# A two-layer hybrid decoder: the weight sums of the last projection made earlier and kept in DRAM, and a written order for all engines in it

## The chip, the core and the metric

The kernel runs on one core of a Trainium2 chip. A core has a tensor engine (PE, whose weight loads the profile lists as PEld), a vector engine (DVE), a scalar engine (ACT), a general engine (POOL) and a queue engine (SP) that here only issues DMAs. The metric is the device time of one execution in microseconds; lower is better.

## The reference

Two layers (`DEPTH` 2) over 1024 tokens of width 1024, in float32:

```
h    = rms_norm(x, pre_gain) * (1 + scale) + shift      # shift, scale, gate from SiLU(c) @ W_mod
proj = h @ w_in                                         # 3088 columns
A    = sliding_window_attention(...) * silu(ag)         # window 128, 8 heads, columns 0..511 of the mix
B    = rms_norm(retention(...)) * silu(rg)              # 4 heads, chunks of 128, columns 512..767
C    = rms_norm(gated_linear_attention(...)) * silu(gg) # 4 heads, columns 768..1023
x    = x + gate * rms_norm(concat(A, B, C) @ w_out, post_gain)
```

Each group of heads carries a state from chunk to chunk in B and C. The layers follow each other, and the last projection, `concat(A, B, C) @ w_out` of the second layer, ends the program.

## The kernel before

**Tiles.** Tokens are taken in 8 tiles of 128. Every matrix product of activations is made in three passes of a high and a low half (`PASSES`), so a product of one tile with a block of 512 rows and 512 columns has 12 matmuls of 128x512. The mix (A, B, C of a tile) is turned and written to DRAM in two halves (`mixS`), and for tiles 2 to 7 of the last layer also unsplit (`mixF`).

**Order of the work.** PE runs in the order in which the program is written (`manual_schedule` over PE). Everything that is not a long product is a *job*, a generator that yields delays. A counter `clk` adds up an assumed cost of the matmuls, and `pump()`, called between groups of matmuls, lets those jobs go on whose delay (from the table `L`) or flag is past. So `L` sets where a job's matmuls stand in PE's order. The other engines get an order from the framework's scheduler, unlike PE. SP's queue works in order, too; a DMA also waits for the one that was issued eight before it on its queue to land.

**The second layer** goes: gate projections, retention (`ret_core`, with the state `stR` on DVE), gated linear attention (`gla_core`, with the state `stG`), window attention in eight pairs of tiles (`attn_run`, `attn_two`: scores to PSUM, softmax on DVE, ACT and POOL in one of four `smx` tiles, transposes, values), the attention's gates (`gate`), and `last_output`.

**The last output.** Tiles 0 and 1 (`PLAIN` = 2) are multiplied block by block. The other six go in three pairs, an even and an odd tile, with seven products a pair instead of eight (a Strassen-like scheme). For it `w_out` is cut in 2 x 2 blocks of 512 x 512. The blocks W00, W10 and W11 are used as they are, and T1 to T4 are sums of blocks. Likewise sums of the two tiles' halves are made (L1430 to L1433) and split in high and low (`msplit`, L157 and L1404). The products of a pair come in the order W00, W10, T2, T1, W11, T3, T4. Results pass through three PSUM banks named `mm` and are added on DVE (L1470) to kept ones (`kept`, L1466 on ACT). Then come the square (L1474), the product with the gate (L1475), and `finish`, which reloads x, adds it (L1373) and stores the output.

**Weight sums.** T1 is made while it is loaded: two loads and a difference (L593) for each of four rows of blocks, `k`. T2, T3 and T4 are made in `sw_second`, a job that starts with the first product of tile 0: four loads, three sums on DVE (L591, L593, L621) and three splits (ACT copies, L157; DVE or POOL differences, L586) for each `k`. Staging tiles `st` are a ring of five.

```
for k in range(4):
    s3, x = sw_load(k, 0, 1), sw_load(k, 1, 1)
    sw_diff(s3, 1, k, x, s3)
    s2, s4 = sw_load(k, 0, 0), sw_load(k, 1, 0)
    eng("sd").tensor_tensor(s2, s3, s2, ALU.add)
    ...
```

Of the kernel before, what the change touches and what calls it, by code (L numbers as in the profile page):

```python
# [14 lines left out]
ALU = mybir.AluOpType  # L15
# [78 lines left out]
def trunk(ctx: ExitStack, tc: tile.TileContext, ins, cst, out):  # L94
# [66 lines left out]
    def dma(k, dst, src):  # L161
        {"S": nc.sync, "A": A, "P": G}[EN[k]].dma_start(dst, src)
# [5 lines left out]
    clk = [0.0]  # L168
    jobs = []
# [100 lines left out]
    srS = dr.tile([NT, P, 256], F32, name="srS")  # L270
    tabS = dr.tile([NP_, P, 2, 256], F32, name="tabS")
# [316 lines left out]
    def sw_diff(dst, i, k, x, y):  # L588

        if i and k > 1:  # L590
            V.scalar_tensor_tensor(dst, x, gnc[:, DEPTH - 1:DEPTH], y, ALU.mult, ALU.subtract)  # L591
        else:
            eng("sd").tensor_tensor(dst, x, y, ALU.subtract)  # L593

    def sw_first(name):
        def conv(k, x, y=None):
            if y is not None:
                sw_diff(x, 0, k, x, y)
# [9 lines left out]
        for k in range(4):  # L608
            if name == "T1":
                request(DEPTH - 1, 2, lambda k=k: (sw_load(k, 0, 1), sw_load(k, 0, 0)), lambda *s, k=k: conv(k, *s))  # L610
            else:
                i, j = int(name[1]), int(name[2])
                request(DEPTH - 1, 1, lambda k=k: (sw_load(k, i, j),), lambda *s, k=k: conv(k, *s))

    def sw_second():
        drain()
        for k in range(4):
            s3, x = sw_load(k, 0, 1), sw_load(k, 1, 1)
            sw_diff(s3, 1, k, x, s3)
            s2, s4 = sw_load(k, 0, 0), sw_load(k, 1, 0)  # L620
            eng("sd").tensor_tensor(s2, s3, s2, ALU.add)  # L621
            sw_split("T2", k, s2, "t2")
            sw_split("T3", k, s3, "t3")
            sw_diff(s4, 1, k, s4, s2)
            sw_split("T4", k, s4, "t4")
            yield L["sw1"]
        for name in ("T2", "T3", "T4"):
            flag(("sw", name))
# [38 lines left out]
    mark = [None] * 4  # L667
# [711 lines left out]
    def prod(dst, a, name, start=True, stop=True, c=slice(0, 512)):  # L1379

        w = sw(name)
        await_flag(("sw", name))
        q = 0
        for i, j in PASSES:
            for k in range(4):
                mult(dst, a[:, i, k, :], w[:, j, k, c], start and q == 0, stop and q == 11)
                q += 1
        pump()

# [11 lines left out]
    def msplit(slot, x, key):  # L1401
        xv = x.rearrange("p (k q) -> p k q", k=4)
        copy("mh" + key, slot[:, 0], xv)
        eng("ml" + key).tensor_tensor(slot[:, 1], xv, f(slot[:, 0]), ALU.subtract)  # L1404

    def slots(b):
        return b[:, :, 0:4, :], b[:, :, 4:8, :]

    class Pair:

        def __init__(self, l, p):
            self.l, self.e, self.o = l, 2 * p, 2 * p + 1

        def parts(self):
            l, e, o = self.l, self.e, self.o
            need_mix(l, e)
            need_mix(l, o)
            self.p = mpart(o, 0), mpart(o, 1), mpart(e, 0), mpart(e, 1)

        def sum(self):  # L1420
            e = self.e
            self.a = []
            for c in range(2):
                s = gp.tile([P, NT * P], F32R, tag=f"kT{c}", name=nm("ma"), bufs=1).rearrange(
                    "p (a k q) -> p a k q", a=2, k=4)
                for a in range(2):
                    dma("lmix", f(s[:, a]), mixS[e, :, a, 4 * c:4 * c + 4])
                self.a.append(s)
            a21, a22, a11, a12 = self.p
            eng("ms0").tensor_tensor(a22, a21, a22, ALU.add)  # L1430
# [404 lines left out]
```

## Time and profile before

| what | value |
|---|---|
| three runs | 992.6, 993.15, 996.84 us; median 993.15 |
| the profiled execution | 1000.45 us, its span 998.7 us |
| granted TensorE clock, mean | 0.982 |
| PE busy | 951.3 us |
| DVE, ACT, POOL busy | 690.3, 414.6, 273.5 us |
| second layer's retention and gated attention | about 590 to 790 us |
| window attention and gates | about 790 to 903 us |
| last output | 898 to 998.7 us; PE's last matmul ends at 991.0 |
| HBM read, written | 109.2 MB, 36.2 MB |

The page lists busy time by engine, then the costliest groups of instructions by source line, with the idle time before them and what ended it. Matmuls are pipelined and their ends are modelled. In the rows of a timeline the bracket names the idle time of the engine before that row and the instruction that ended it; `L173` and `L188` are helpers in which all matmuls and transposes are recorded, `L157` and `L159` one for copies, `L162` one for DMAs.

### The profile page before, as it was taken

Reading aid. Unit: us, or ns where it says so; the run is one execution under the profiler, and the core shown is the slowest. Engines: PE = TensorE matmul, PEld = TensorE weight load, DVE = VectorE, ACT = ScalarE, POOL = GpSimd, SP = SyncE. Lnnn points to the kernel's source line nnn. Section 1 sums busy time; section 2 is a strip of 40 time slices with the busy share of each in tenths; the row PEclk is TensorE's granted clock in tenths of the full one; section 3 lists DMA queues with packets and bytes.
Section 4 is the critical chain, followed back from the end, with each engine's and each line's share of the span. In section 5 each row is a group of like instructions: output and inputs, shape, how many; then the busy total and the mean of one; then the engine's idle time right before and its main releaser. Section 6 shows DMA issues by size and latency. Waiting matters only on the chain. (4 is left out here: it accounts for less than half of the span.)

```text
span 998.7 us, 19555 instructions
## 1 busy us (share of the span) xinstructions
PE 951.3 (95%) x7117; PEld 829.5 (83%) x7117; DVE 690.3 (69%) x1679; ACT 414.6 (42%) x1160; POOL 273.5 (27%) x302
## 2 busy tenths in 40 slices
PE   5788999999999999999999999999999998999796
PEld 1687999988998877878889999998899876777575
DVE  4788956857756777755677385785766568866876
ACT  3677521223332556633455431133333256663322
POOL 1776101222430234420123010122331034634001
PEclk9899999989999999999999999999999999999899
DMA  9742623433326255687455150361223324587874
GB/s 296 272 129 81 189 73 103 135 97 94 117 83 183 71 171 165 187 272 257 164 172 170 59 165 32 118 179 65 68 78 101 111 86 133 163 267 206 263 240 143
DMA packets 129968, 148.76 MB, mean 149 GB/s; under 512 B 14112, under 2 KB 94284, under 8 KB 129872
## 3 DMA queue, kind: packets, MB, share of 16 engines
q1 hardware_dynamic: 124176, 137.96, 45.5%
q10 hardware_dynamic: 5696, 9.56, 2.6%
q8 instruction: 56, 0.92, 0.4%
q14 instruction: 40, 0.33, 0.1%
HBM read 109.20 MB, written 36.18 MB: 146 GB/s over the span
## 5 line engine op out<-in xcount | busy, mean ns | idle before, releaser
L173 PE MATMUL mm<-arena,arena 128*128 128x256 f32 (+2 forms) x2880 | 463.6, 316 | 4.4 <-POOL arena L553 1.4
L173 PEld LDWEIGHTS mm<-arena,arena 128*128 128x128 f32 x2880 | 401.7, 190 | 38.6 <-ACT arena L722 2.5
L657 POOL TENSOR_TENSOR sm<-sm,mhalf 128x1 f32<-128x1 f32 (+1 forms) x64 | 55.4, 867 | 326.4 <-DVE sm L656 320.0
L173 PE MATMUL mm<-arena,mx 128*128 128x512 f32 (+1 forms) x564 | 130.6, 388 | 6.2 <-ACT kept L1466 4.8
L173 PE MATMUL mm<-arena 128*128 128x256 f32 (+2 forms) x768 | 126.7, 317 | 6.2 <-DVE arena L723 3.4
L173 PEld LDWEIGHTS mm<-arena,mx 128*128 128x128 f32 x564 | 103.2, 191 | 28.6 <-ACT kept L1466 5.3
L173 PEld LDWEIGHTS mm<-arena 128*128 128x128 f32 x768 | 108.7, 191 | 16.4 <-DVE arena L723 4.1
L553 POOL TENSOR_TENSOR arena<-st,arena 128x512 fp32r<-128x512 f32 x34 | 51.0, 1503 | 104.0 <-ACT arena L157 93.1
L157 ACT ACTIVATE t<-aux 128x512 f32<-128x512 f32 (+2 forms) x108 | 52.0, 506 | 57.1 <-PE aux L188 34.2
L157 ACT ACTIVATE arena<-st 128x512 fp32r<-128x512 f32 x94 | 56.1, 627 | 43.5 <-DMA st<-in_w_in_dram 16.0
L1051 POOL TENSOR_TENSOR smx<-smx,sm 128x512 f32<-128x512 f32 x32 | 34.6, 1082 | 127.2 <-DVE sm L1050 123.6
L553 DVE TENSOR_TENSOR arena<-st,arena 128x512 fp32r<-128x512 f32 x74 | 59.4, 818 | 6.1 <-ACT arena L157 4.5
L1047 ACT ACTIVATE smx<-smx,sm 128x129 f32<-128x129 f32 x128 | 49.9, 393 | 21.1 <-DVE sm L1044 20.8
L366 DVE SCALAR_TENSOR_TENSOR acc<-st,c_act,acc 128x512 f32<-128x512 f32 x60 | 45.9, 764 | 16.2 <-DMA st<-in_w_mod_dram 15.9
L1100 ACT ACTIVATE t<-aux 128x256 f32<-128x256 f32 x32 | 12.3, 384 | 86.6 <-PE aux L173 80.8
L173 PEld LDWEIGHTS aux<-t,mx 32*128 32x128 f32 (+1 forms) x896 | 39.8, 187 | 4.3 <-issue 2.4
L173 PE MATMUL aux<-t,mx 32*128 32x32 f32 (+1 forms) x896 | 41.0, 272 | 0.2 <-DVE modg L380 0.2
L716 ACT ACTIVATE t<-aux,mod,mod 128x128 f32<-128x128 f32 x76 | 29.1, 459 | 22.1 <-PE aux L188 7.7
L188 PE MATMUL aux<-c_ident,t 128*128 128x128 f32 (+1 forms) x228 | 37.6, 274 | 0.0
L1373 DVE SCALAR_TENSOR_TENSOR t<-t,sm,t 128x512 f32<-128x512 f32 x32 | 23.0, 747 | 19.0 <-DMA t<-in_x_dram 10.8
L1105 DVE TENSOR_TENSOR t<-aux,sm 128x256 f32<-128x256 f32 x32 | 13.6, 425 | 29.7 <-POOL sm L657 29.7
L157 ACT ACTIVATE t<-mm 128x256 f32<-128x256 f32 x40 | 14.8, 379 | 40.2 <-PE mm L173 27.1
(236 smaller groups left out, 1455.0 us busy)
## 6 DMA issues: line engine op xcount, KB each, us to landing
st<-in_w_in_dram SPq DMA_DIRECT2D x96, 256.0 KB
st<-in_w_mod_dram SPq DMA_DIRECT2D x64, 256.0 KB
st<-in_w_out_dram SPq DMA_DIRECT2D x52, 256.0 KB
mx<-mixS SPq DMA_DIRECT2D x20, 512.0 KB
mixS<-t SPq DMA_DIRECT2D x72, 128.0 KB
wm<-in_w_mod_dram SPq DMA_DIRECT2D x12, 512.0 KB
t<-tabS SPq DMA_DIRECT2D x16, 256.0 KB
aoS<-t SPq DMA_DIRECT2D x32, 128.0 KB
```

The lines of the kernel that those rows point to most:

```text
L157: A.activation(dst, src, AF.Copy)
L173: T.matmul(dst, lhsT, rhs, start=start, stop=stop)
L188: T.transpose(dst, src, idn)
L366: V.scalar_tensor_tensor(acc, wt, c_act[:, k:k + 1], acc, ALU.mult, ALU.add)
L553: e.tensor_tensor(lo, st, f(hi), ALU.subtract)
L657: mark[1] = G.tensor_tensor(r, r, mhalf[:, :w], ALU.pow)
L716: A.activation(hf[:, ks], x[:, ks], AF.Identity, scale=gain, bias=shift)
L1047: A.activation(sm[:, h, :], sm[:, h, :], AF.Exp, bias=mx[:, h:h + 1], accum_out=sums[:, h:h + 1])
L1051: eng("pn").tensor_tensor(sm[:, :, 0:128], sm[:, :, 0:128], rs.unsqueeze(2).to_broadcast((P, 4, P)), ALU.mult)
L1100: A.activation(sq, po, AF.Square)
L1105: V.tensor_tensor(h4(g1), h4(po), r.unsqueeze(2).to_broadcast((P, 4, 64)), ALU.mult)
L1373: V.scalar_tensor_tensor(xt[j], yg[j], r, xt[j], ALU.mult, ALU.add)
```

## The change

T1 to T4 are made in a new job `sw_sums` during the second layer's retention and gated attention, in the `smx` tiles, which the window attention uses later. For each `k` it loads four blocks of `w_out`, makes four sums on DVE and stores them in DRAM (`twS`). Its loads are ordered behind the last mix DMA recorded before them (`issue_after`). T1 and the others are then loaded as one finished block for each `k`. In `last_output` the order of ACT, DVE, POOL and SP is also the written one. Its steps (sums and splits of tiles, squares, products with the gate, ends of tiles, splits of weights) are jobs with delays of their own; loads of x are issued when a tile's end begins; products call `pump()` after every four matmuls. The delays of the second layer's attention, retention state and gates are others. The high and low parts of the gated attention output for tiles 4 to 7 and of the odd tile's right half lie in smaller tiles (`t1`).

```
+    def sw_sums():
+        yield L["su1"]
...
+        for k in range(4):
+            q = []
+            for n, (i, j) in enumerate(((0, 1), (1, 1), (0, 0), (1, 0))):
+                q.append(gp.tile([P, 4, 129], F32, tag="smx", ...))
...
+                with tc.issue_after(mark[2].ins):
+                    dma("lw", q[n], w_out[DEPTH - 1, r:r + P, 512 * j:512 * j + 512])
+                yield L["su2"]
+            b12, b22, b11, b21 = q
+            yield L["su3"]
+            less(b22, b22, k, b12)
+            yield L["su4"]
+            eng("su").tensor_tensor(b12, b12, b11, ALU.subtract)
+            yield L["su4"]
+            dma("sw", twS[0, k], b12)
+            eng("su").tensor_tensor(b11, b22, b11, ALU.add)
+            yield L["su4"]
+            dma("sw", twS[2, k], b22)
+            less(b21, b21, k, b11)
+            yield L["su4"]
+            dma("sw", twS[1, k], b11)
+            dma("sw", twS[3, k], b21)
...
         for k in range(4):
-            if name == "T1":
-                request(DEPTH - 1, 2, lambda k=k: (sw_load(k, 0, 1), sw_load(k, 0, 0)), lambda *s, k=k: conv(k, *s))
+            if name[0] == "T":
+                n = int(name[1]) - 1
+                request(DEPTH - 1, 1, lambda k=k: (sw_sum_load(n, k),), lambda *s, k=k: conv(k, *s))
...
+        def weights():
+            drain()
+            blocks = [(n, k) for n in (1, 2, 3) for k in range(4)]
+            sts = []
+            for i in range(len(blocks) + 4):
+                if i < len(blocks):
+                    sts.append(sw_sum_load(*blocks[i]))
...
+        def end(t, n=2):
+            xt = [t2(), t2()]
+            for j in range(2):
+                sl = slice(512 * j, 512 * j + 512)
+                dma("lx", xt[j], xs[t, :, sl])
+            yield L["e1"]
+            for i in range(2):
+                yield (0.0, ("yg", t, i))
...
+            def sums(self):
+                yield L["p1"]
+                a21, a22, a11, a12 = self.x
+                eng("ms0").tensor_tensor(a22, a21, a22, ALU.add)
...
+                yield (0.0, ("free", self.p, 0))
+                self.s[2], self.s[1] = slots(mix_tile())
+                job(self.part(2, a11, "0"))
...
+        job(mod_all(l, (2,)))
+        if l == DEPTH - 1:
+            job(sw_sums())
...
         if l == DEPTH - 1:
-            last_output(l, load_mix)
+            E = mybir.EngineType
+            with tc.manual_schedule(engines={E.Activation, E.DVE, E.Pool, E.SP}):
+                last_output(l)
...
-"aq1@1": 9.8, "aq7@1": 10.56, "ag1@1": 4.95, "aq2@1": 1.02, "aq6@1": 6.8, "aq5@1": 6.15, "rc1@1": 0.37, "rc4@1": 1.99, "lay1@1": 1.7
+"aq1@1": 6.5, "aq7@1": 8.06, "ag1@1": 6.85, "aq2@1": 3.52, "aq6@1": 7.2, "aq5@1": 6.05, "rc1@1": 0.57, "rc4@1": 4.49, "lay1@1": 1.5
```

SP has 642 rows before and 672 now: 8 block loads fewer from `w_out`, 16 stores to `twS`, 16 loads from it, and 6 more for the odd tile's halves, which are loaded in quarters. The sums on DVE are 16 before and 16 now.

What stands where, at three places. The first is ACT in the last output, at the copy of W00 of the first pair (`kept<-mm`); `mx` are the split sums of the pair's tiles, `sq` or `st` with `sm` a square with its sum, `arena` a weight block. Before:

```order
L1474 ACTIVATE st_11413,sm_11250<-t_1982_11251 128x512
L157 ACTIVATE mx_11447<-t_2015_11418 128x512
L157 ACTIVATE mx_11447<-t_2016_11420 128x512
L162 DMA out_dram<-t_2022_11439 128x512
L157 ACTIVATE mx_11527<-t_2017_11422 128x512
L162 DMA out_dram<-t_2023_11440 128x512
L157 ACTIVATE mx_11527<-t_2014_11416 128x512
L1466 ACTIVATE kept_11559<-mm_11546 128x512
```

And now:

```order
L157 ACTIVATE mx_11542<-t_2005_11361 128x512
L157 ACTIVATE arena_72<-st_11491 128x512
L1455 ACTIVATE sq_11558,sm_11515<-t_2042_11540 128x512
L157 ACTIVATE mx_11542<-t_2002_11355 128x512
L157 ACTIVATE arena_72<-st_11510 128x512
L1601 ACTIVATE kept_11572<-mm_11548 128x512
```

Before, all four splits of the pair and the two stores of tile 0 stand right ahead of the copy; now the two splits of the second slot do, and the first two splits stand further up.

DVE at the pair's sums. Before, `st` are weight sums, `aux_11332` and `mm_11395` the two results of tile 0, and L1430 and L1431 the first sums of the pair's tiles:

```order
L591 SCALAR_TENSOR_TENSOR st_11381<-st_11381,gnc,st_11379 128x512
L1470 TENSOR_TENSOR t_1983_11252<-aux_11332,kept_11328 128x512
L1475 TENSOR_TENSOR t_1983_11252<-t_1983_11252,modg_7102 128x512
L1712 SCALAR_TENSOR_TENSOR t_2011_11408<-t_1961_11155,t_2011_11408 128x512
L1470 TENSOR_TENSOR t_1982_11251<-mm_11395,kept_11328 128x512
L1712 SCALAR_TENSOR_TENSOR t_2012_11410<-t_1977_11240,t_2012_11410 128x512
L1475 TENSOR_TENSOR t_1982_11251<-t_1982_11251,modg_7102 128x512
L662 TENSOR_TENSOR sm_11434<-sm_11250 128x1
L656 TENSOR_SCALAR sm_11436<-sm_11434 128x1
L1430 TENSOR_TENSOR t_2015_11418<-t_2014_11416,t_2015_11418 128x512
L1431 TENSOR_TENSOR t_2014_11416<-t_2016_11420,t_2014_11416 128x512
```

And now (L1518 to L1521 are the pair's sums, L1440 the results of tile 0):

```order
L1801 TENSOR_TENSOR t_2011_11388<-t_1993_11307,t_2010_11387 128x256
L1548 TENSOR_TENSOR arena_72<-st_11336,arena_72 128x512
L1518 TENSOR_TENSOR t_2003_11357<-t_2002_11355,t_2003_11357 128x512
L1519 TENSOR_TENSOR t_2002_11355<-t_2004_11359,t_2002_11355 128x512
L1520 TENSOR_TENSOR t_2004_11359<-t_2003_11357,t_2004_11359 128x512
L1521 TENSOR_TENSOR t_2005_11361<-t_2005_11361,t_2004_11359 128x512
L1440 TENSOR_TENSOR t_2014_11417<-aux_11363,kept_11329 128x512
L1548 TENSOR_TENSOR arena_72<-st_11376,arena_72 128x512
L1440 TENSOR_TENSOR t_2020_11443<-mm_11420,kept_11329 128x512
```

The pair's sums moved ahead of the results of tile 0, and the weight sums are gone.

The second place is DVE in the second layer's retention, at a rotation of q (`t_1334`, before `t_1332`), the masked scores (`c_causal`) and the state's update (`stR`). Before:

```order
L940 TENSOR_TENSOR t_1332_7671<-t_1332_7671,tr_7672 128x4x32
L1282 TENSOR_TENSOR t_1332_7671<-t_1332_7671,c_qdec 128x256
L1304 TENSOR_TENSOR t_1337_7693<-aux_7687,c_causal 128x2x128
L1304 TENSOR_TENSOR t_1337_7693<-aux_7688,c_causal 128x2x128
L1102 TENSOR_REDUCE sm_7713<-t_1341_7711 128x4
L1323 TENSOR_TENSOR stR<-stR,aux_7703 64x2x64 x2
```

And now:

```order
L970 TENSOR_TENSOR t_1334_7676<-t_1334_7676,tr_7677 128x4x32
L601 TENSOR_TENSOR su_7671<-su_7671,su_7630 128x512
L1312 TENSOR_TENSOR t_1334_7676<-t_1334_7676,c_qdec 128x256
L1334 TENSOR_TENSOR t_1339_7698<-aux_7692,c_causal 128x2x128
L1334 TENSOR_TENSOR t_1339_7698<-aux_7693,c_causal 128x2x128
L616 TENSOR_TENSOR su_7630<-su_7630,su_7726 128x512
L1353 TENSOR_TENSOR stR<-stR,aux_7708 64x2x64 x2
```

Two of the block's four sums (`su`) came in, one inside the rotation and one ahead of the state's update.

The third place is PE where the window attention ends (`va` and `vd` are values, `mm_11158` and now `mm_11259` the last gate product, `mm_11249` and now `mm_11314` W00 of tile 0). Before:

```order
L173 MATMUL mm_11158<-arena_72 128x512 x8
L173 MATMUL mm_11249<-arena_302,mx_11243 128x512 x12
L173 MATMUL mm_11282<-arena_302,mx_11246 128x512 x12
L173 MATMUL aux_11298<-t_1968_11201,va_9706 64x256 x2
L173 MATMUL aux_11298<-t_1969_11203,vd_11010 64x256 x2
L173 MATMUL aux_11298<-t_1971_11210,va_9740 64x256 x2
L173 MATMUL aux_11298<-t_1972_11212,vd_11014 64x256 x2
L173 MATMUL aux_11332<-arena_465,mx_11243 128x512 x24
```

And now:

```order
L176 MATMUL aux_11207<-t_1964_11137,va_9753 64x256 x2
L176 MATMUL aux_11207<-t_1965_11139,vd_10955 64x256 x2
L176 MATMUL aux_11207<-t_1967_11146,va_9789 64x256 x2
L176 MATMUL aux_11207<-t_1968_11148,vd_10959 64x256 x2
L176 MATMUL mm_11198<-arena_72 128x512 x16
L176 MATMUL mm_11259<-arena_72 128x512 x24
L176 MATMUL mm_11314<-arena_303,mx_11311 128x512 x12
L176 MATMUL mm_11338<-arena_303,mx_11331 128x512 x12
L176 MATMUL aux_11363<-arena_466,mx_11311 128x512 x24
```

The last values moved from behind W00 of tiles 0 and 1 to 40 gate matmuls ahead of it.

379 lines of the change are left out of this document (202 added, 177 removed).

## The prediction

> All times are those of the one profiled execution unless a median is named. A change below about 5 us (0.5%) cannot be told from no change by timing this kernel: its three runs lie 4 us apart.
>
> **What bounds the kernel now.** I read the profile's page first, for the engine that is never free. It is the tensor engine (PE):
>
> ```profile
> PE 951.3 (95%) x7117; PEld 829.5 (83%) x7117; DVE 690.3 (69%) x1679; ACT 414.6 (42%) x1160; POOL 273.5 (27%) x302
> ```
>
> So the span is PE's work plus PE's idle time, and what the change can win is idle time of PE alone. Next I asked who PE waits for, in the four stretches from 600 us on, which hold all that the change touches (a row has the total in us, the times, the longest; the first two rows are 600 to 700, then one for 700 to 800, one for 800 to 900, and two for 900 to the end):
>
> ```profile
> PE aux L173 <- ACT t L157: 0.2, 1, 0.2
> PE aux L173 <- DVE modg L380: 0.2, 1, 0.2
> PE aux L173 <- DVE sm L656: 0.6, 1, 0.6
> PE aux L188 <- DVE smx L1040: 3.3, 3, 2.1
> PE mm L173 <- ACT kept L1466: 4.8, 1, 4.8
> PE mm L173 <- DVE t L1470: 3.0, 3, 1.7
> ```
>
> In retention and gated attention (600 to 790) PE waits 1.0 us in all, in the window attention 3.3, in the last output 7.8. Then the last output in order of time on PE (start, length, line, bracketed idle time before):
>
> ```profile
> 921.93 2.88 PE L173 MATMUL mm<-arena,ma 128*128 128x512 f32 x12
> 926.53 3.01 PE L173 MATMUL mm<-arena,ma 128*128 128x512 f32 x12 [1.72 <-DVE t L1470]
> 934.40 5.33 PE L173 MATMUL mm<-arena,mx 128*128 128x512 f32 x12 [4.85 <-ACT kept L1466]
> ...
> 956.92 2.98 PE L173 MATMUL mm<-arena,mx 128*128 128x512 f32 x12 [0.72 <-DVE t L1470]
> ...
> 976.94 2.98 PE L173 MATMUL mm<-arena,mx 128*128 128x512 f32 x12 [0.60 <-DVE t L1470]
> ...
> 987.92 3.05 PE L173 MATMUL mm<-arena,a 128*128 128x256 f32 x24
> ```
>
> Each row of 12 is one product of a pair of tiles. 921.93 is W00 of the first pair, 926.53 its W10, 934.40 its T2. The same T2 takes 2.98 in the next pair and 5.33 here, after the longest wait. The stages say why: the granted clock (column after the engines) is 0.51 there.
>
> ```profile
> 934.40:939.50 5.10, 5.10 (x12) 4.04 (x13) 4.01 (x10) 1.34 (x4) 0.56 (x1) 0.51 0.76 201
> ```
>
> So the idle time of the last output costs 1.72 + 4.85 + 0.72 + 0.60 = 7.9 us, and the slow clock behind the 4.85 another 5.33 - 2.98 = 2.35: 10.2 us.
>
> Why T2 waits: its PSUM bank is one of three, and it held W00's result until ACT had copied it. That product was done before 925; the copy started at 933.76. ACT works in order, and ahead of the copy stand four splits of the pair's sums, the last of them at 933.23:
>
> ```profile
> 933.23 0.63 ACT L157 ACTIVATE mx<-t 128x512 fp32r<-128x512 f32 x1 [0.37 <-DVE t L1373]
> 933.76 0.58 ACT L1466 ACTIVATE kept<-mm 128x512 f32<-128x512 f32 x1
> ```
>
> The splits wait for DVE, which makes the sums (L1430 to L1433) from 928.14 on, because until 922 it stood in the weight sums, waiting for their loads:
>
> ```profile
> 913.07 0.75 DVE L591 SCALAR_TENSOR_TENSOR st<-st,gnc,st 128x512 f32<-128x512 f32 x1 [3.11 <-DMA st<-in_w_out_dram]
> ...
> 919.38 1.26 DVE L621 TENSOR_TENSOR st<-st,st 128x512 f32<-128x512 f32 x1 [1.70 <-DMA st<-in_w_out_dram]
> ...
> 928.14 0.69 DVE L1430 TENSOR_TENSOR t<-t,t 128x512 f32<-128x512 f32 x1
> ...
> 931.46 0.68 DVE L1433 TENSOR_TENSOR t<-t,t 128x512 f32<-128x512 f32 x1
> ```
>
> **The change part by part.**
>
> *Weight sums out of the last output, and the order there.* The 12 sums of `sw_second` and their 16 loads become 12 loads of finished blocks and 12 splits. DVE then has the pair's sums ahead of the first result of tile 0 (the new order of DVE), which PE cannot deliver before about 911 (24 matmuls of T1 and W11). They are over 17 us earlier than 928. The copy of W00 (new order of ACT) stands behind two splits that wait for tile 1's slot, which PE frees with W10 of tile 1, right before 921.93, behind a square of that tile and two weight splits; five rows of some 0.6, so the copy can follow W00 at once, near 925. That removes 4.85 and, with it, the 2.35 of slow clock. What is late next for T2: its sum row on DVE that frees the bank of tile 1's W10. It stands behind the final addition of tile 0, which needs the reload of x. I put that reload's landing well ahead of 920, since its DMA now stands before the last five weight loads on SP; T2 would want the bank near 927. The 1.72, 0.72 and 0.60 are the same kind of wait (a DVE row L1470 that frees a bank). In the steady pairs DVE has about 27 rows, 23 of them near 0.61 us apart, some 14.5 us of the 19 us that PE's seven products of 2.72 take. That fits but is not loose, and all engines now follow a written order, in which a late load holds all behind it. I take 10.2 removed, and put 1.5 back for new waits: near the 0.60 to 1.72 of the waits that are there now. The ends are 0 and 5.1 (half of it back).
>
> *A half clock may count less.* The Trainium skill ("TensorE: Matmul & The Clock Gate", Part 1: The HAM clock gate) says that PE drops to half clock after an idle window of about 3.4 us and comes back after as long a busy one. By that a long wait costs 1.7 us more, against the 2.35 of the rows; the estimated sum would be 0.65 us smaller in gain. The rows decide, since the 0.51 lasted through all twelve matmuls.
>
> *Window attention.* The delays of the second layer change (`aq1`, `aq7`, `aq2`, `ag1`), so that PE starts the score pairs closer together and the last values are multiplied before W00, not behind it (the order of PE). The wait of 3.3 us is for PSUM banks: transposes that follow the next pair's scores closely, before DVE has copied these:
>
> ```profile
> 826.69 1.70 PE L173 MATMUL aux<-kT,mx 64*128 64x256 f32 x24
> ...
> 834.36 1.09 PE L188 MATMUL aux<-c_ident,smx 128*128 128x128 f32 x8 [2.05 <-DVE smx L1040]
> ```
>
> The new order has more PE work between those two, so the wait should shrink; but the same softmax work of ACT, DVE and POOL now falls into a shorter time. I take 2.3 of the 3.3 as gone; the ends are all of it gone and 2 us more than before.
>
> *Sums in retention.* 16 operations of 128x512 on DVE: 12 at the 0.69 of the row at 928.14, and 4 at the 0.76 of L591, 11.3 us; the same count leaves the end of the layer. Beside them 16 loads and 16 stores of 256 KB enter SP's queue. There DVE and the DMA engines have room (columns: PE, PEld, DVE, ACT, POOL, clock, DMA share, GB/s):
>
> ```profile
> 600.00:700.00 100.00, 99.61 (x846) 92.47 (x845) 65.78 (x191) 25.61 (x65) 19.50 (x22) 0.98 0.33 98
> 700.00:800.00 100.00, 99.43 (x993) 90.42 (x992) 64.25 (x202) 34.92 (x114) 24.22 (x34) 1.00 0.29 89
> ```
>
> DVE goes from 65% to about 71% there. The danger is order: the loads are queued behind the stores of finished mix tiles on SP, and a sum that waits for its load holds the rotations and the retention state (`stR`) behind it, for which PE waits. The row at 913.07 shows such a wait: 3.11. Behind it stands `rc4`, longer by 2.5 us, which puts the state's matmuls later in PE's row. The cost lies between -1.0 (the waits of now vanish) and 4 x 3.1 = 12.4 (one such wait in each of the four blocks reaches PE whole). I take +1.0, near what PE waits there now.
>
> *DVE beside POOL.* The sum at 919.38 took 1.26 instead of 0.69, while POOL ran this:
>
> ```profile
> 917.16 2.93 POOL L586 TENSOR_TENSOR arena<-st,arena 128x512 fp32r<-128x512 f32 x2 [1.29 <-ACT arena L157]
> ```
>
> The Trainium skill ("GPSIMD Engine Reference", 1. Specifications) says that POOL shares its SBUF interfaces with DVE and contends with DVE instructions that have two SBUF inputs. That speaks against the new place, where POOL works on gated attention; the trace agrees in this row. Were every sum as slow as that row, 16 x 1.26 = 20.2 us would go into DVE there, 8.9 more than I count; DVE would still be at 75%, so it brings the slower rival below nearer and leaves my sum.
>
> *Tail.* In the last rows the final scale of the odd tile is now recorded behind the additions of the even tile and the gain products:
>
> ```profile
> 991.41 0.41 DVE L1470 TENSOR_TENSOR t<-mm,kept 128x256 f32<-128x256 f32 x1
> 991.74 0.74 DVE L1373 SCALAR_TENSOR_TENSOR t<-t,sm,t 128x512 f32<-128x512 f32 x1
> ...
> 994.11 1.41 DVE L1373 SCALAR_TENSOR_TENSOR t<-t,sm,t 128x512 f32<-128x512 f32 x2 [0.44 <-POOL sm L657]
> ```
>
> Between the last half's addition (991.41) and the scale of POOL, which the pair at 994.11 waits for, stood one addition of the even tile (0.74). Now two stand there, and one product more (near the 0.41 of the half): +1.2. The ends are 0.5 and 2.
>
> **Sum.** -10.2 + 1.5 - 2.3 + 1.0 + 1.2 = -8.8, against the profiled execution's own 1000.45 us. That stands 7.3 us over the median of 993.15. As part of the waits hangs on landings of DMAs, which may be shorter without the profiler, I take 0.8 off: -8.0, a median of 985.2.
>
> **Rivals.**
> *Only half (B).* The written order makes new waits in the last output: a blocked row of ACT or DVE, or SP's queue, in which the pair's tiles now stand behind weight blocks that wait for their staging buffer. For it: DVE's 14.5 of 19 us, and loads that take as long as the one below (a reload of x, from the chain that ended last). Against it: the tiles of a pair are asked for a whole pair ahead. 5.1 of the 10.2 would come back instead of 1.5: 993.15 - 8.0 + 3.6 = 988.8, and with a second such wait of 3.67 some 992.5.
>
> ```profile
> 968.01 3.67 DMA t<-xs
> ```
>
> *The profile overstates it (C).* The loads on which DVE waits at 913 and 919 land sooner in the timed runs, the 4.85 and 2.35 are small there, and little is to be won: 993.15 - (8.8 - 7.2) = 991.6. For it speaks the 7.3 us between profile and median; against it, that the order of ACT would still hold the copy.
>
> *Retention pays (A, slower).* The weight sums hold DVE in each of the four blocks, and PE waits for `stR` or a rotation. At its full price of 12.4 instead of 1.0 the sum is +3.4 over mine of the other terms: 993.15 - 8.0 + 11.4 = 996.6. It turns the sign once more than 9.0 us reach PE. Against it: DVE is idle a third of that time, and PE waits 1.0 us there now.
>
> **How the numbers follow.** Forecast 0.60 (its own range 980 to 988), B 0.20, C 0.08, A 0.12. If every cost but the tail vanishes, the time is 993.15 - 10.2 - 3.3 - 1.0 + 1.2 = 979.9, the lower end. The upper end takes in B and C and what of A is not at its full price: 993. Faster by over 0.5% (under 988.2): the forecast and a quarter of B, 0.65. Slower (over 998.1) needs A and B together (996.6 + 3.6) or longer waits than A's: 0.08. The rest, 0.27, lies within 0.5%.
>
> **What would show it.** Right: no wait of PE over 2 us from W00 on, the clock there at 1.0, the copy of W00 within 1 us of its product, tile sums of the first pair before 912, waits on softmax under 1.5 us, PE's end to the span's end about 9 us (7.7 now). Wrong: a wait of PE on `kept` or on the sum rows of the same size as before; waits of several us on `stR` or rotations between 590 and 790; DVE waiting for loads of `su`; SP holding `ma` or x loads behind weight blocks.

## The result, and the profile after

| | kernel before | changed kernel |
|---|---|---|
| median of six runs each, on one chip | 994.09 us (992.6 to 998.69) | 987.44 us (984.14 to 988.61) |
| the profiled execution | 1000.45 us, span 998.7 | 988.42 us, span 986.7 |
| last matmul ends | 990.97 | 978.58 |

The ratio is 0.9923, 95% interval 0.9896 to 0.9950: faster by 0.8%. Forecast were 985.2 us, between 979.9 and 993.0.

The page after, busy time by engine. PE's share is up by one point and its instructions are as many as before; DVE's work is the same, only elsewhere.

```profile
PE 946.8 (96%) x7117; PEld 830.5 (84%) x7117; DVE 689.1 (70%) x1681; ACT 415.6 (42%) x1160; POOL 267.2 (27%) x300
```

PE's waits after, in three stretches: three rows for 600 to 700 us, two for 700 to 790, one for 790 to 900. From 900 us to the end the view has no row at all, where before there were 7.8 us.

```profile
PE aux L176 <- DVE stR L1355: 1.4, 1, 1.4
PE aux L176 <- ACT t L157: 1.1, 1, 1.1
PE aux L176 <- DVE t L1123: 0.4, 1, 0.4
PE aux L191 <- ACT t L1260: 1.4, 1, 1.4
PE aux L176 <- DVE sm L687: 0.7, 1, 0.7
PE aux L176 <- ACT t L157: 0.5, 1, 0.5
```

So PE's wait in the window attention went from 3.3 to 0.5 us, and in retention and gated attention it went from 1.0 to 5.0. The last output after, PE in order of time (904.83 is T1 and W11 of tile 0; 921.15 is W00 and W10 of the first pair; 926.59 its T2, which had waited 4.85 us and taken 5.33; 975.55 the last product):

```profile
904.83 5.60 PE L176 MATMUL aux<-arena,mx 128*128 128x512 f32 x24
...
921.15 5.60 PE L176 MATMUL mm<-arena,ma 128*128 128x512 f32 x24
926.59 2.88 PE L176 MATMUL mm<-arena,mx 128*128 128x512 f32 x12
...
975.55 3.03 PE L176 MATMUL mm<-arena,t 128*128 128x256 f32 x24
```

Nothing stands in brackets any more. From 904.83 to the end of the last product at 978.58 there are 73.8 us. The stage has 27 products, and one takes 2.72 us, which is the step from one such row to the next (T2 at 926.59, T1 at 929.31): together 73.4. So this stage cannot get shorter by less waiting.

DVE after, at the same place: the sums of the pair's tiles (first and last row of four), the first addition of x, which waits for its load, and the addition behind it, which frees the bank that T2 takes:

```profile
908.71 0.68 DVE L1518 TENSOR_TENSOR t<-t,t 128x512 f32<-128x512 f32 x1
...
910.88 0.69 DVE L1521 TENSOR_TENSOR t<-t,t 128x512 f32<-128x512 f32 x1
...
921.63 0.75 DVE L1478 SCALAR_TENSOR_TENSOR t<-t,sm,t 128x512 f32<-128x512 f32 x1 [2.31 <-DMA t<-xs]
...
923.57 0.69 DVE L1440 TENSOR_TENSOR t<-mm,kept 128x512 f32<-128x512 f32 x1
```

The sums stand at 908.7 instead of 928.1. The x load was late by 2.31 us, as feared, and with it the bank of T2; yet the addition at 923.57 has ended 2.3 us before T2 starts at 926.59. ACT's copy of W00 (`kept`) is not prompt either. It starts 3.6 us behind the product (921.15 + 2.72). ACT stood until 923.65 before a split that waited for a weight block from `twS`, and the squares and splits behind that split then filled it up to the copy:

```profile
923.65 0.63 ACT L157 ACTIVATE arena<-st 128x512 fp32r<-128x512 f32 x1 [6.70 <-DMA st<-twS]
...
927.51 0.57 ACT L1601 ACTIVATE kept<-mm 128x512 f32<-128x512 f32 x1
```

That costs nothing now: T2 started before the copy, so its bank is not W00's any more. Had it been, T2 would have waited for the copy's end at 928.08, some 1.5 us (an estimate from these rows).

**Where the time went, by three marks on PE.** A is the first row of scores of the first layer's window attention; up to it every engine has the same order of work in both kernels. B is T1 of tile 0, before which all of the window attention is done in both. C is the end of the last matmul. For the kernel before, A and B, then A for the changed one (its B is the first row of the fence on the last output; C comes from the last rows of PE, 987.92 + 3.05 and 975.55 + 3.03):

```profile
326.16 1.65 PE L173 MATMUL aux<-kT,mx 64*128 64x128 f32 x24
...
905.48 5.73 PE L173 MATMUL aux<-arena,mx 128*128 128x512 f32 x24
```

```profile
322.82 1.65 PE L176 MATMUL aux<-kT,mx 64*128 64x128 f32 x24
```

A differs by 3.3 us between the two executions, though nothing ahead of it was changed. In all the profiles of this study it lies between 319.9 and 326.2. Between A and B some executions have one or two short stretches of half clock (last section), 1.7 us each; I take them off. Then the stages repeat to 0.7 us in the two executions of the kernel before and to 0.3 in three of the changed one, and can be compared more finely than the timed medians. Each row is still one execution: the sums of the three stages agree with the timed ratios to about 3 us, and not better.

| kernel, profiled execution | A to B, less half clock | B to C | C to end | ratio to before, 95% interval |
|---|---|---|---|---|
| before | 577.6 | 85.5 | 7.7 | |
| before, second execution | 577.7 | 84.8 | 7.7 | |
| changed | 578.6 | 73.8 | 8.1 | 0.9923 (0.9896 to 0.9950) |
| changed, second execution | 578.6 | 73.8 | 8.2 | 0.9909 (0.9884 to 0.9933) |
| changed, third (experiment 10) | 578.3 | 73.8 | 8.1 | 0.9891 (0.9871 to 0.9910) |
| sums alone | 583.5 | 82.8 | 7.8 | 1.0045 (1.0028 to 1.0063) |
| delays alone | 577.9 | 85.2 | 7.7 | 1.0031 (1.0013 to 1.0049) |
| written order and delays | 578.0 | 88.1 | 8.1 | 1.0049 (1.0030 to 1.0068) |
| sums and written order | 582.4 | 77.9 | 8.1 | 0.9967 (0.9944 to 0.9990) |
| the same with the state's new delays | 581.0 | 78.1 | 8.1 | 0.9975 (0.9957 to 0.9993) |
| sums and delays | 578.3 | 78.7 | 8.1 | 0.9970 (0.9950 to 0.9991) |
| changed, without the sums | 575.9 | 73.8 | 8.1 | 0.9881 (0.9859 to 0.9903) |
| changed, a sum behind the state | 576.5 | 73.8 | 8.1 | 0.9870 (0.9847 to 0.9894) |
| changed, block loads on ACT's queue | 584.3 | 73.8 | 8.2 | 0.9991 (0.9974 to 1.0008) |

Against the mean of the two executions before, the change wins 11.4 us in the last output, loses 1.0 ahead of it and 0.4 in the tail: 10.0 us with the half-clock stretches taken off. From A on, the first profiles of the two kernels lie 8.7 us apart as they stand, with two such stretches in the changed one and one in the one before. Timed were 7.7 us (0.9923) and 9.1 (0.9909); the plain medians lie 6.7 and 8.6 apart.

### The profile page after: what moved, and what is told of

It reads as the page before. It is cut to its first block, busy times and chain, and to the rows that moved or that the text cites. A ratio compares the mean times of both kernels' runs of the same rounds, so it can differ in the third digit from the quotient of the medians.

```text
span 986.7 us, 19637 instructions
## 1 busy us (share of the span) xinstructions
PE 946.8 (96%) x7117; PEld 830.5 (84%) x7117; DVE 689.1 (70%) x1681; ACT 415.6 (42%) x1160; POOL 267.2 (27%) x300
## 5 line engine op out<-in xcount | busy, mean ns | idle before, releaser
L176 PE MATMUL mm<-arena,mx 128*128 128x512 f32 (+1 forms) x564 | 128.0, 383 | 0.0
L191 PEld LDWEIGHTS aux<-c_ident,t 128*128 128x128 f32 (+1 forms) x228 | 27.1, 141 | 6.4 <-issue 2.0
```

Source lines behind the costliest of these rows:

```text
L176: T.matmul(dst, lhsT, rhs, start=start, stop=stop)
L191: T.transpose(dst, src, idn)
```

## The experiments

The question was which part brought it: the sums, the written order, or the delays. And whether the stall of T2, on which the forecast stood, was there in every execution.

**1. Sums alone.** The kernel before, with `sw_sums` and finished blocks.

```
+        if l == DEPTH - 1:
+            job(sw_sums())
...
+                request(DEPTH - 1, 1, lambda k=k: (sw_sum_load(n, k),), ...)
 # last_output, its order and L[...@1] as before
```

> The kernel before with one half of the change: the weight sums are made in retention and kept in DRAM, T1 to T4 are loaded as finished blocks; the last output keeps its old order and its old steps, and the delays of the second layer are the old ones. Theory 'sums' (DVE's late tile sums were the whole cause of the stall of T2): the 4.85 us wait and the slow clock of 2.35 us go, retention pays some 4 us as in the changed kernel, so 994 - 7 + 4 = 991 us, and the sums of the first pair of tiles on DVE start before 915 us. Theory 'order' (ACT's copy behind four splits is the cause): the copy is still behind them, the stall stays, and the sums cost 4 us: 998 us. Theory 'profile overstates' (the stall was only in that one execution): between 994 and 998 us.

Measured: 1000.26 us against 996.35, ratio 1.0045. PE in retention and in the last output:

```profile
674.49 0.63 PE L176 MATMUL aux<-stR,t 128*128 128x128 f32 x2 [3.49 <-DVE sm L687]
...
928.84 3.01 PE L176 MATMUL mm<-arena,mx 128*128 128x512 f32 x12
...
946.13 5.04 PE L176 MATMUL mm<-arena,a 128*128 128x512 f32 x10 [5.65 <-ACT arena L157]
```

The stall of T2 (at 928.84) is gone, as theory "sums" has it (the pair's sums start at 919.0 us, later than it said). Its bank is not W00's here either, for it starts before the copy has ended:

```profile
928.82 0.58 ACT L1496 ACTIVATE kept<-mm 128x512 f32<-128x512 f32 x1
```

With W00's bank T2 would have waited some 0.6 us (an estimate from the two rows), so of what was won at T2 the earlier copy is most, and the other bank the rest. But only 2.4 us were won in the stage (82.8 against the mean of 85.2 before). T4 waits 5.65 us in T2's place, for its own weight blocks. In the scheduler's order on SP the loads of the last two stand behind the loads of the next pair's tiles (`ma`), and are issued only when T4 is due:

```profile
935.56 4.95 SPq L162 DMA_DIRECT2D ma<-mixS  x4
940.60 0.86 SPq L162 DMA_DIRECT2D st<-twS  x2
```

T4 also runs at a lower clock (5.04 for ten matmuls). And A to B lost 5.8 us (583.5 against 577.7). The largest wait there is the 3.49 us of the first row: with the old delay PE reaches the state's matmul while DVE still stands in the sums and waits for loads of `su`. So "sums" named the cause of the old stall rightly and its price wrongly.

**2. Written order and delays, sums late.** The changed kernel with the 16 block loads, 12 sums and 12 splits in `weights()`.

```
-            job(sw_sums())
...
+            for k in range(4):
+                s3, x = sw_load(k, 0, 1), sw_load(k, 1, 1)
+                s2 = sw_load(k, 0, 0)
+                yield L["sw1"]
+                sw_diff(s3, 1, k, x, s3)
...
+                sw_split("T4", k, s4, "t1")
```

> The changed kernel with the weight sums made late, as before: 16 loads of blocks, 12 sums on DVE and 12 splits in the last output, T1 made from two loads; the written order of all engines, the new steps and the new delays stay. Theory 'sums': DVE again stands in weight sums and waits for their loads when the sums of the first pair are due; as the order is written, these waits hold the rows behind them, and the time is 991 to 995 us though retention gets its 4 us back. Theory 'order': the stall stays away, retention's 4 us are won, and the time is about 983.5 us.

Measured: 1002.16 us, ratio 1.0049, slower than both theories said. PE waits for the weights of T2:

```profile
928.20 0.80 PE L176 MATMUL mm<-arena,mx 128*128 128x512 f32 x1 [3.99 <-ACT arena L157]
937.02 3.81 PE L176 MATMUL mm<-arena,mx 128*128 128x512 f32 x9 [8.03 <-ACT arena L157]
```

The pair's sums are in time here, since their place is written ahead; it is the weights that are late by 12.0 us. The 12 sums and 12 splits here have fixed places behind 16 loads that pass through the ring of five staging tiles. Other places for these late sums might do better; only this one was measured. In the places given, there is room for finished blocks and not for sums, and that is what the early sums buy.

**3. Sums and delays, order left to the scheduler.**

```
-            with tc.manual_schedule(engines={E.Activation, E.DVE, E.Pool, E.SP}):
-                last_output(l)
+            last_output(l)
```

> The changed kernel, but in the last output ACT, DVE, POOL and SP get their order from the framework's scheduler, as before; all else is the changed kernel's. Theory 'sums': with the weight sums gone the order hardly matters, within 1.5 us of the changed kernel's 987.4. Theory 'order': the scheduler puts rows that free PSUM banks behind others again, waits of 3 us or more stand ahead of products, and the time is 990 to 994 us.

Measured: 993.3 us, ratio 0.9970; theory "order" holds. B to C is 78.7 instead of 73.8. PE, then DVE, at the first pair:

```profile
928.26 4.36 PE L176 MATMUL mm<-arena,mx 128*128 128x512 f32 x12 [3.35 <-DVE t L1440]
```

```profile
926.62 0.90 DVE L1457 TENSOR_TENSOR t<-t,modg 128x512 f32<-128x512 f32 x1 [0.85 <-ACT sq L1455]
927.43 0.68 DVE L1440 TENSOR_TENSOR t<-mm,kept 128x512 f32<-128x512 f32 x1
```

The addition that frees T2's bank stands behind a product with the gate that waits for a square. In the written order it stands ahead of that product, at 923.57.

**4. Sums and written order, the nine old delays.**

```
-"aq1@1": 6.5, "aq7@1": 8.06, "ag1@1": 6.85, "aq2@1": 3.52, ... "rc4@1": 4.49, "lay1@1": 1.5
+"aq1@1": 9.8, "aq7@1": 10.56, "ag1@1": 4.95, "aq2@1": 1.02, ... "rc4@1": 1.99, "lay1@1": 1.7
```

> The changed kernel with the nine old delays of the second layer (window attention, gates and retention state). Theory 'attention pays as forecast' (2.3 to 2.8 us of PE's waits on the softmax go by the delays): 989.7 to 990.5 us, with waits of PE on softmax rows of 3 us again between 790 and 900 us. Rival, that the delays do nothing by themselves: 987.4 us. Rival, that the later state update (rc4) is what made retention 4 us slower: under 986 us, with the retention waits gone.

Measured: 993.01 us, ratio 0.9967: 4 to 6 us lost against the changed kernel, more than any of the three theories had. Part is ahead of the last output (582.4 against 578.6 from A to B). The waits in retention did not go: PE waits longest at the state's matmul:

```profile
673.03 0.46 PE L176 MATMUL aux<-stR,t 128*128 128x128 f32 x2 [2.88 <-DVE sm L687]
```

The extra is in the last output, 77.9 instead of 73.8. DVE and PE there:

```profile
912.50 0.69 DVE L1518 TENSOR_TENSOR t<-t,t 128x512 f32<-128x512 f32 x1 [5.00 <-DMA t<-mixF]
```

```profile
929.28 4.57 PE L176 MATMUL mm<-arena,mx 128*128 128x512 f32 x12 [2.17 <-DVE t L1440]
```

With the old delays the last values of the attention follow W00, and what ends the attention (its gates, stores and loads of mix tiles) stands later on DVE and SP. The tiles of the first pair land later, DVE's sums with them (912.50 instead of 908.71), and all rows behind, down to the addition that T2 waits for.

**5. The same with the two state delays new.** Only the seven delays of attention and gates are old (`rc1`, `rc4` stay new).

> The changed kernel with seven of the nine old delays, those of window attention and gates; the two of the retention state (rc1, rc4) stay new. Theory 'the attention's delays carry it': its end falls behind W00 again, the loads of the first pair's tiles and DVE's sums come some 4 us later, T2 waits 2 us at a lower clock, and the softmax waits are back: all of the loss of the run with nine old delays (4.4 us against the changed kernel), ratio about 0.9965. Rival 'the state's delays carry it': ratio at 0.9915, with the nine's loss due to the wait of 2.9 us on a head norm (sm) in retention.

Measured: 994.0 us, ratio 0.9975. PE at the state's matmul, and T2, which waits again:

```profile
677.04 0.46 PE L176 MATMUL aux<-stR,t 128*128 128x128 f32 x2 [1.19 <-DVE stR L1355]
...
930.39 4.44 PE L176 MATMUL mm<-arena,mx 128*128 128x512 f32 x12 [2.31 <-DVE t L1440]
```

The attention's delays carry the loss in the last output (78.1). The state's two are worth 1.4 us from A to B (582.4 to 581.0), which the timing cannot tell.

**6. Delays alone.** The kernel before with the nine new values.

> The kernel before with the nine new delays alone; weight sums and last output as before. Theory 'the parts need each other': attention ends before W00 and its waits shrink by 2 to 3 us, but DVE still stands in weight sums, and the stall of T2 stays or grows by what attention wins, so the ratio is 0.997 to 1.002. Rival 'the delays pay by themselves': 4 us as in the changed kernel, ratio 0.996 or less.

Measured: 998.99 us, ratio 1.0031, slightly slower than expected. PE's wait in the attention is 2.0 us, against 3.3 and 2.6 in the two executions of the kernel before, and T2's stall grows to 6.69:

```profile
932.67 5.26 PE L173 MATMUL mm<-arena,mx 128*128 128x512 f32 x12 [6.69 <-ACT st L1474]
```

Nothing is won: A to B is 577.9 (577.7 before) and the last output 85.2 (the mean before). So "the parts need each other" holds. The stages do not show the 3 us by which the timing is slower; where these lie stays open. What is left of the attention's wait hangs on T1: DVE waits for a load of its difference, with the softmax and ACT's copies behind it, and PE waits for the copies (in experiment 2, where T1 is made in the same way, 1.29 us at the same place):

```profile
842.76 0.69 DVE L593 TENSOR_TENSOR st<-st,st 128x512 f32<-128x512 f32 x1 [2.62 <-DMA st<-in_w_out_dram]
...
850.04 1.46 PE L173 MATMUL aux<-kT,mx 64*128 64x256 f32 x12 [1.42 <-ACT t L157]
```

**7. The kernel before once more.**

> The kernel before, unchanged, for a second profiled execution. Theory 'steady stall': T2 of the first pair waits between 4 and 6 us for the copy of W00 and runs at a lower clock again, since the order of ACT is fixed. Rival 'profile overstates': the weight loads land sooner here, the wait is under 2.5 us, and the execution is some 5 us shorter than the 1000.45 us of the first profile.

Measured: 996.35 us, span 994.6. PE at W10 and T2 of the first pair:

```profile
923.36 4.61 PE L173 MATMUL mm<-arena,ma 128*128 128x512 f32 x12 [1.95 <-DVE t L1470]
931.22 5.49 PE L173 MATMUL mm<-arena,mx 128*128 128x512 f32 x12 [3.26 <-ACT kept L1466]
```

T2 waits less, but W10 runs slow too. The waits of the stage are 5.4 us, and the two slow rows cost 4.6 + 5.5 - 2 x 2.9 = 4.3; that is 9.7 together, against 10.2 in the first profile. The wait of T2 alone lies between the two theories, but the length of the stage is steady (84.8 and 85.5), so "overstates" falls. The 4.1 us between the two spans are 1.75 ahead of A, 1.7 of half clock and 0.7 here.

**8. The changed kernel once more.**

> The changed kernel once more, unchanged, as the measure for the three kernels beside it and as a second profiled execution. Theory 'steady': no wait of PE from W00 on in this execution either, retention waits of about 5 us again with DVE waiting some 5 us for a load of su, ratio to before 0.990 to 0.9945. Rival 'luck of one execution': PE waits of 2 us or more in the last output in this profile, where the first profile had none.

Measured: 986.14 us against 994.76, ratio 0.9909; again no wait from 900 us on, and 4.4 us in retention and gated attention. "Steady" holds.

**9. Without the sums.** T1 to T4 are loaded as plain blocks of `w_out`, and `sw_sums` is left out.

```
-            job(sw_sums())
...
-        dma("lw", st, twS[n, k])
+        dma("lw", st, w_out[DEPTH - 1, r:r + P, 512 * j:512 * j + 512])
```

> The changed kernel without the weight sums: nothing is loaded, added or stored for them in retention, and in the last output T1 to T4 are loaded straight from blocks of w_out (so the odd products use wrong weights). It prices the sums in retention. Theory 'the sums cost retention what PE waits more there': 4 us faster than the changed kernel, with PE's waits between 600 and 790 us back at about 1 us. Rival 'free': within 1 us of the changed kernel; then the waits there come from the delays and not from the sums.

Measured: 984.73 us, ratio 0.9881. PE's waits between 600 and 790 us are 2.1, and A to B is 575.9: the sums cost 2.7 us of PE, not the 4 of the first theory, and not nothing. Of the 5.0 us of waits in the changed kernel some are there without them.

**10. Sums later.** `su3` 12 instead of 6, `su4` 4.3 instead of 5.8.

> The changed kernel with the first sum of each block recorded 12 instead of 6 us after its loads (and the sums 4.3 instead of 5.8 apart, so that the whole takes as long as before). Theory 'DVE is held by a sum that waits for its load': DVE's waits on su go from 9.1 us to under 2, PE's wait on stR (1.4 us) goes, and the kernel is 1.5 to 2.5 us faster than the changed kernel. Rival 'other DVE work is in the way': the loads are waited for no more, PE waits as before on transposes' results and on ACT's and DVE's copies, and the time stays within 1 us.

Measured: 984.54 us, ratio 0.9891, and DVE still waits for the load:

```profile
672.90 0.69 DVE L601 TENSOR_TENSOR su<-su,su 128x512 f32<-128x512 f32 x1 [4.78 <-DMA su<-in_w_out_dram]
```

The delays moved nothing: apart from one store on SP, all five engines have the order of the changed kernel, since DVE follows the scheduler there and not the table. Neither theory was tested by it. So this was a third execution of the changed kernel (578.3, 73.8, 8.1), and it shows how far a ratio moves by itself: 0.9923, 0.9909, 0.9891.

**11. Loads on ACT's queue.**

```
-                with tc.issue_after(mark[2].ins):
-                    dma("lw", q[n], w_out[...])      # SP
+                dma("lsu", q[n], w_out[...])         # ACT
```

> The changed kernel with the 16 block loads of the sums issued by ACT's queue instead of SP's, so that they stand behind no store of a mix tile. Theory 'SP's queue makes the loads late': DVE's waits on su under 2 us and 1.5 to 2.5 us faster than the changed kernel, less what 16 issues of some 0.4 us cost ACT. Rival 'the landing itself is slow' (other transfers share the DMA engines): DVE still waits 5 us at the second block and the time stays within 1 us; or ACT, held by an issue that waits for its buffer, makes it slower.

Measured: 993.38 us, ratio 0.9991. The edit also took away the order behind the last mix DMA, and the scheduler moved all 16 loads and the sums into the first layer. ACT's row there, and the stretch from 400 to 500 us (busy us of PE, PEld, DVE, ACT, POOL; then clock, DMA share, GB/s):

```profile
456.54 0.60 ACT L1366 ACTIVATE t<-mm 128x512 f32<-128x512 f32 x1 [4.88 <-DMA twS<-su]
```

```profile
400.00:500.00 100.00, 92.93 (x498) 74.03 (x497) 60.84 (x123) 35.54 (x107) 19.02 (x27) 0.98 0.89 289
```

ACT stood 4.88 us in an issue that waited for its buffer (the row that follows it has the bracket), and PE waited 7.1 us in a stretch in which it waits in no other profile. A to B is 584.3, and the last output is as short as in the changed kernel (73.8). Whether SP's queue makes the loads late is not answered by it. Queue and place changed together, so neither is priced alone; with both, the sums in the first layer take back what the last output wins.

**12. A sum behind the state.** The first sum of each block is ordered behind the last update of the retention state on DVE.

```
-            V.tensor_tensor(stR, stR, cdt..., ALU.mult)
+            mark[3] = V.tensor_tensor(stR, stR, cdt..., ALU.mult)
...
-            less(b22, b22, k, b12)
+            with tc.issue_after(mark[3].ins):
+                less(b22, b22, k, b12)
```

> The changed kernel with the first sum of each block ordered behind the latest update of the retention state on DVE (and the delays of the sums as in the run before, 12 and 4.3). The delays alone left DVE's order as it was; this moves the sum of the second block behind the state update that it held. Theory 'a sum that waits for its load holds the state': the wait of PE on stR (1.0 to 1.4 us) goes, and the time is 1 to 1.5 us under the changed kernel, ratio to before 0.988 to 0.990. Rival 'the next row is held instead' (a head norm or a rotation stands behind the sum now): the wait moves to another row of the same size and the ratio stays at 0.991.

The place in the changed kernel, DVE and PE:

```profile
673.64 0.69 DVE L601 TENSOR_TENSOR su<-su,su 128x512 f32<-128x512 f32 x1 [5.25 <-DMA su<-in_w_out_dram]
...
675.87 0.42 DVE L1355 TENSOR_TENSOR stR<-stR,c_cdt 128x256 f32<-128x256 f32 x1
```

```profile
676.43 0.46 PE L176 MATMUL aux<-stR,t 128*128 128x128 f32 x2 [1.35 <-DVE stR L1355]
```

and in this one, DVE:

```profile
671.12 0.42 DVE L1356 TENSOR_TENSOR stR<-stR,c_cdt 128x256 f32<-128x256 f32 x1
...
673.35 0.69 DVE L601 TENSOR_TENSOR su<-su,su 128x512 f32<-128x512 f32 x1 [0.48 <-DMA su<-in_w_out_dram]
```

Measured: 984.36 us against 996.75, ratio 0.9870 (0.9847 to 0.9894), the lowest of all kernels. The first theory holds: PE has no wait on `stR`, and A to B is 576.5, 2.1 us less than the changed kernel and 0.6 over the one without sums. A later wait for a copy of ACT (L1260, here L1261) fell with it, from 1.41 to 0.70 us. The load lands no sooner; only what stood behind it has moved. Against the kernel before it is faster beyond doubt; against the changed kernel the trace says 2.1 us, and the intervals of the ratios overlap.

## Why the prediction was right, and where its steps were not

The forecast of -8.8 us against the profiled execution stands beside -8.7 from A on. Most of that is right mechanism, but the closeness is luck: the last output won 2.7 us more than forecast, and what stands ahead of it lost 1.0 where a gain of 1.3 was forecast. The median of 985.2 also stood on three runs of the kernel before that were low (993.15; its later medians, of 6 to 31 runs, are 994.09 to 996.75).

- **Last output: -10.2 + 1.5 = -8.7 forecast, -11.4 measured.** The cause is shown by taking single parts away: early sums free DVE, the written order has the bank free in time, and T2 neither waits nor slows. The written order alone, with late sums and old delays, was not run. The 1.5 put back for new waits was a mis-sized term: nothing came back. The other 1.2 are rows that ran a little longer (2.98 and 3.01 where 2.88 stands now) and such losses that the list of waits leaves out.
- **Which part did it.** I gave the whole 10.2 to sums and order. Experiments 4 and 5 show that 4 us of the win (77.9 and 78.1 against 73.8) hang on the attention's delays, through the time at which the first pair's tiles land. I had read these delays for the attention's own wait only.
- **ACT's copy.** "The copy can follow W00 at once" failed: it came 3.6 us later. T2 did not need it, since its bank is freed by an addition on DVE, and that was in the prediction too (the sum row that frees the bank of tile 1's W10). The reload of x, which that row stands behind and which was put well ahead of 920, was there at 921.63: late, but not too late.
- **Window attention and retention: -2.3 + 1.0 = -1.3 forecast, +1.0 measured.** Without the sums A to B wins 1.8 us (577.7 to 575.9), so the -2.3 was nearly right. It needs T1 as a finished block, which the prediction did not say: with the delays alone A to B is +0.2, and a wait of 2.0 us is left in the attention (experiment 6). The sums cost 2.7 instead of 1.0. Rival A's mechanism (a sum that waits for its load holds the state) is there, in one of four blocks, at 5.25 us of DVE and about 2 us of PE (experiment 12). The state's two new delays (`rc1`, `rc4`) hide a part: at the state's matmul PE waited 3.49 and 2.88 us with the old ones (experiments 1 and 4), and 1.35 and 1.19 with the new ones.
- **Tail: +1.2 forecast, +0.4 measured.** The rows stand as said, and they cost what was said: from the half's addition to POOL's scale there were 1.68 us (991.41 to 993.09) and are now 2.94. The other 0.8 came back where nothing was forecast: the addition starts 0.05 us behind PE's end instead of 0.44, and the scale takes 0.54 instead of 0.98. DVE and POOL after, and POOL before:

```profile
978.63 0.42 DVE L1440 TENSOR_TENSOR t<-mm,kept 128x256 f32<-128x256 f32 x1
...
981.57 0.54 POOL L688 TENSOR_TENSOR sm<-sm,mhalf 128x1 f32<-128x1 f32 x1 [3.47 <-DVE sm L687]
```

```profile
993.09 0.98 POOL L657 TENSOR_TENSOR sm<-sm,mhalf 128x1 f32<-128x1 f32 x1 [1.61 <-DVE sm L656]
```

- **0.8 us for the profiler, and rival C.** No run shows that landings are shorter without the profiler, and the 7.3 us between profile and median need no such reason. The stall is no effect of one execution (experiment 7); against the second profile the first was long mainly ahead of A (1.75 us) and by a stretch of half clock (1.7).
- **Rival B** (half comes back) did not happen in the changed kernel. It did in the kernels with a part missing: T2 or T4 waits 2 to 12 us when the order, the delays or the sums are taken away.

The Trainium skill's rule on the clock gate ("TensorE: Matmul & The Clock Gate", Part 1: The HAM clock gate) gave 1.7 us for the slow clock behind the long wait. The traces agree with it elsewhere (last section, 1.7 each), while behind the stalls of T2 the loss was 2.35 and, with W10 and T2 slow, about 4.3. In the first of these the granted clock was 0.50 from 933 to 939 us, for longer than the 3.4 us from which the 1.7 come.

## What to carry to other kernels

A stall that shows at one row can be held by several causes in series, so that taking one away uncovers the next a few us later: here the delays or the sums alone lost 3 to 4.5 us, order and delays lost 5, the other two pairs won 3, and all three together won 8 to 11. Before costing a move of work, look for every queue in which a landed result is still waited for, and order the row that waits for a load behind the rows that others need: in experiment 12 that won 2.1 us though the load came no sooner. To compare kernels whose runs scatter by 5 us, cut the trace at instructions that have the same work ahead of them in both, and compare the stages.

## What the runs showed of the hardware

The clock fell to half without a wait of several us. In the kernel before, after a wait of 0.16 us among 56 matmuls of 32 rows by 32 columns from 690.47 to 692.72, the next row of twelve matmuls took 4.62 us (PE, then two us of it: the granted clock, 0.50, is the third number from the end):

```profile
691.05 1.41 PE L173 MATMUL aux<-t,mx 32*128 32x32 f32 x41 [0.16 <-DVE modg L380]
...
692.72 4.62 PE L173 MATMUL mm<-arena,arena 128*128 128x512 f32 x12
```

```profile
694.00:696.00 2.00, 2.00 (x7) 1.52 (x6) 0.39 (x1) 0.00 (x0) 0.00 (x0) 0.50 0.03 9
```

In experiment 10 the same twelve ran at full clock, behind a wait of 0.37 us at the same place:

```profile
691.47 3.01 PE L176 MATMUL mm<-arena,arena 128*128 128x512 f32 x12
```

Each such stretch lost 1.7 us (the mean granted clock from 690 to 700 us was 0.83), and there were none, one or two between A and B in an execution. Most stood at the small matmuls of gated attention. Others stood behind a wait, in retention (the 3.49 us of experiment 1: clock 0.50 from 674.7 to 678), in the attention or, in experiment 11, in the first layer; a kernel that waits more can have more of them, and taking them off hides that. The Trainium skill, in the page and section named above, says that half clock follows an idle window of about 3.4 us that runs freely, not from the kernel's start. The length agrees (1.7 lost is 3.4 at half), and so does that one order shows it in one execution and not in the next. No wait of 3.4 us stands ahead of the rows above, though, nor ahead of W10 in experiment 7 (1.95 us of wait, then 4.61 instead of 2.88) or T2 in experiment 5 (2.31, then 4.44). A stretch that is idle in part, or filled with small matmuls, seems to count as idle. That is argued from these rows, not tried.
